# Half of a shift vector moved to another engine and another time, a release order changed, and a last norm split over three engines

## The chip, the cores and the metric

The kernel runs on one core of a Trainium2 chip. Five engines work side by side, each with a queue of its own: PE (TensorE: matrix products), DVE (VectorE), ACT (ScalarE), POOL (GpSimd) and SP (SyncE, which here only issues loads and stores). The metric is device time in microseconds (us), lower is better; executions of one kernel agree closely, and about 0.2% is what can be told from no change.

## The reference

One layer of a hybrid encoder block on 256 tokens of width 2048, all in float32, and a final norm. Cut to what matters:

```python
mod = silu(c) @ w_ada + b_ada                     # 2048 x 12288
sh1, sc1, gt1, sh2, sc2, gt2 = split(mod, 6)
h = rms_norm(x, g_mix) * (1 + sc1) + sh1
qa, ka, va, qb, kb, vb = split(h @ w_in)          # 2048 x 4608
o = concat[rms_norm(attention_A), rms_norm(attention_B)]   # 16 heads each
x = x + gt1 * (o @ w_out)                         # 2048 x 2048
h = rms_norm(x, g_ffn) * (1 + sc2) + sh2
# top-1 of 4 groups, then top-2 of its 8 experts, for each token
y = sum over experts of combine[:, e] * ((silu(h @ w_gate[e]) * (h @ w_up[e])) @ w_down[e])
x = x + gt2 * y
shf, scf = split(silu(c) @ w_ada_final + b_ada_final, 2)   # 2048 x 4096
out = rms_norm(x, g_final) * (1 + scf) + shf
```

Heads of B have a bias by relative position. There are 32 experts, each with three matrices of 4.2 MB.

## The kernel before

**The ring.** All large weights come through one ring of six SBUF buffers of 2.1 MB (`Ring`). The tiles are listed in the order of use; SP issues the loads in that order, and a load waits until the buffer released six tiles before is free. Buffers are freed by PE (products done) or by DVE (sums done), in program order.

**Stages, in order of time.** (1) The first two mod vectors with the first part of W_in, about 0 to 160 us. (2) W_in: twelve steps (`in_step`), each with one tile of w_in (64 or 32 products on PE, about 14 us) and, by the table `VECTOR_TILES`, two further tiles of w_ada or w_ada_final. These extra tiles are worked off on DVE: a vector times a 2048 x 1024 block is 16 scalar_tensor_tensor operations of 128 x 1024 (`vec_step`, L385), four to a tile, into an accumulator that ones-products on PE add up over the partitions later (`vec_finish`, L404). (3) W_out: eight steps (`out_step`) with two halves t = 0, 1 of 16 products each, again with extra tiles. The attention is woven in: `weave(n)` starts n heads' scores, transposes the heads of the weave before and does the value products of the one before that. In W_in a step has `weave(0)` and `weave(2)`; in W_out each half has `weave(2)`. For B a head pair's bias strip is loaded on ACT's queue (`bias_B`), and POOL sets a corner of it (L454) before it scales the heads' probabilities (L494, L495). All heads must be done before W_out's step 4. (4) Routing: router products, second norm (`rsqrt_mean`, L190 to L198, with its Sqrt on ACT, L192), a chain of small DVE operations, then the first gather (L780). (5) MoE: eight groups of four experts. Each group has 16 tiles of gate and up and 8 of down; a group's result is scattered back (`scatter`, L863) while the next group runs. After group 0 a branch (`further_rounds`) is there for experts with more than 32 tokens; it isn't taken with these inputs. (6) The final norm and the output.

**The vector shf** (the first half of w_ada_final's columns, 16.8 MB) is made on PE: its columns 0 to 1535 in eight tiles of 1.6 MB, six before the routing (`shift_step` into the bank `shift`, copied at L692) and two before group 0's experts (`shift_b`); its last 512 columns in three tiles at the very end (`last_block`), behind the last w_down tile. The output of columns 0 to 1535 is normalized and stored before that last block, the rest after it.

**Scatters after group 0** stand before the branch, those of the other groups in the next group's steps. Group 7's w_down tiles hold 128 rows by 1024 columns of four experts.

Of the kernel before, what the change touches and what calls it, by code (L numbers as in the profile page):

```python
# [38 lines left out]
VECTOR_TILES = [2, 2, 2, 2, 2, 2, 2, 2, 2, 2, 2, 2, 2, 2, 2, 2, 3, 3, 2, 0]  # L39
# [45 lines left out]
def block_kernel(ctx: ExitStack, tc: tile.TileContext, a: dict):  # L85
# [25 lines left out]
    for name, w, col in (("gt1", ada, 2 * D), ("sh2", ada, 3 * D), ("sc2", ada, 4 * D), ("gt2", ada, 5 * D), ("scf", fin, D)):  # L111
        for c in (0, 1024):
            vec_tiles += [((name, c // 512), k, 4, 1024, rows(w, k * 512, 4, col + c, 1024)) for k in range(4)]
# [11 lines left out]
    shf_tiles = [ring.add((2, 1536), rows(fin, 256 * i, 2, 0, 1536)) for i in range(8)]  # L125
# [3 lines left out]
    for g in range(8):  # L129
# [18 lines left out]
    last_block = [(c0, c1, ring.add((c1 - c0, 512), rows(fin, c0 * 128, c1 - c0, 1536, 512))) for c0, c1 in ((0, 8), (8, 14), (14, 16))]  # L148

# [61 lines left out]
    with ExitStack() as sa:  # L211
# [384 lines left out]
        def out_step(i, idx):  # L596
# [8 lines left out]
            for t in range(2):  # L605
# [15 lines left out]
                weave(2)  # L621
# [53 lines left out]
        def shift_step(pm, i, last):  # L675
            w = ring.get(shf_tiles[i])
            for k in range(2):
                for J in range(3):
                    PE.matmul(
                        pm[32 * J : 32 * J + 32, :], lhsT=cact[:, 2 * i + k : 2 * i + k + 1].to_broadcast([128, 32]),  # L680
                        rhs=w[:, k, J * 512 : (J + 1) * 512], start=k == 0 and i in (0, 6), stop=k == 1 and i == last, skip_group_check=True,
                    )
            ring.release(shf_tiles[i])

        shift = bank("s", "shift")
        shift_step(shift, 0, 5)
        router_turns(3)
        shift_step(shift, 1, 5)
# [57 lines left out]
        V.tensor_copy(cnt, pp[0:1, 64:96])  # L746

# [59 lines left out]
    def turned(pw, name):  # L807
# [3 lines left out]
        sm = pb.tile([128, SEQ], F32, tag="smat", name=f"smat_{name}")  # L811
# [40 lines left out]
    def gated(yp, ch, name):  # L852
        ys = pb.tile([128, 2, 512], F32, tag="ys", name=f"ys_{name}{ch}")
        for n in range(2):
            c = ch * 1024 + n * 512
            V.tensor_tensor(ys[:, n, :], yp[n], gt2bc[:, c : c + 512], op=ALU.mult)  # L856
        return ys

# [36 lines left out]
    def further_rounds():  # L895

        with tc.If(nc.values_load(most[0:1, 0:1], min_val=0, max_val=2) > 0):
            pke = pb1.tile([128, 2], F32, name="pke")
            cbe = pb1.tile([128, 2], F32, name="cbe")
            with tc.For_i(0, 8, 1) as g, tc.If(nc.values_load(busy[0:1, bass.ds(g, 1)], min_val=0, max_val=2) > 0), tc.For_i(g * 4, g * 4 + 4, 1) as e:  # L900
# [4 lines left out]
                with tc.For_i(0, n_e, 1) as _:  # L905
# [7 lines left out]
                    smf = turned(pwf, "f")  # L913
# [12 lines left out]
                    for ch in range(2):  # L926
# [11 lines left out]
                        scatter(smf, gated(ypf, ch, "f"), ch, "f")  # L938


    four = pb1.tile([128, 2], F32, name="four")
    V.tensor_reduce(four[:, 0:1], ident[:, 0:128:32], axis=AX.X, op=ALU.add)
# [3 lines left out]
    shift = mbank("y", "shift_b", 4)  # L946
    for i in range(6, 8):
        shift_step(shift, i, 7)
    shf_b = pb1.tile([128, 512], F32, name="shf_b")
    S.copy(shf_b[0:96, :], shift[0:96, :])  # L950

# [14 lines left out]
    for g in range(8):  # L966
# [8 lines left out]
        else:  # L975
            for J in range(4):
                steps[(3, 4, 5, 6)[J]].append(lambda J=J: spread([R["gt2"]], ROW_ADA + 20, gt2bc, (J,)))
# [45 lines left out]
        else:  # L1023
            S.activation(four[:, 1:2], four[:, 0:1], AF.Sqrt)
            rl = pb1.tile([128, 512], F32, tag="act", name="rl")
            for ch in range(2):
                yp = [mbank("y", f"yp{g}{ch}{n}", 4) for n in range(2)]
                for fc in range(4):
                    w = ring.get(dn[ch * 4 + fc])
                    down(yp, aT, lambda e: w[:, e, :], fc)  # L1030
                    ring.release(dn[ch * 4 + fc])
                    if fc == 1 and ch == 1:
# [3 lines left out]
                    if fc == 1 and ch == 0:  # L1036
                        shbc = new_xg("shbc").rearrange("p k n -> p (k n)")
                        spread([R["shf"][0:96], shf_b[0:96]], ROW_FIN, shbc, range(3))
                pending.append((sm, gated(yp, ch, f"g{g}"), ch, f"g{g}", True))
        if g == 0:  # L1040
            for job in pending:
                scatter(*job)
            pending = []
            further_rounds()

    tail = mbank("u", "tail", 1)
    PE.matmul(tail, lhsT=pick(ROW_FIN + 3, 128), rhs=pr, start=True, stop=False)  # L1050
    for job in pending:
        scatter(*job)
# [4 lines left out]
    for t in range(2):  # L1057
        for n in range(3):
            c = slice(n * 512, (n + 1) * 512)
            V.scalar_tensor_tensor(big[:, t, c], big[:, t, c], r3[:, t : t + 1], shbc[:, c], op0=ALU.mult, op1=ALU.add)  # L1060
        nc.sync.dma_start(out=out[:, t, 0:1536], in_=big[:, t, 0:1536])
    part = mbank("y", "part", 4)
    for c0, c1, idx in last_block:
        w = ring.get(idx)
        for c in range(c0, c1):
            if c < 14:
                q = 32 * (c % 4)
                PE.matmul(
                    part[q : q + 32, :], lhsT=cact[:, c : c + 1].to_broadcast([128, 32]), rhs=w[:, c - c0, :],
                    start=c < 4, stop=c >= 10, skip_group_check=True,  # L1070
                )
            else:
                PE.matmul(tail, lhsT=cact[:, c : c + 1].to_broadcast([128, 128]), rhs=w[:, c - c0, :], start=False, stop=False)
        ring.release(idx)
        if c1 == 14:
            sums = pb.tile([128, 2, 512], F32, tag="ys", name="sums")[:, 0, :]
            S.copy(sums, part)
    PE.matmul(tail, lhsT=four[:, 0:1].to_broadcast([128, 128]), rhs=sums, start=False, stop=True)
    for t in range(2):
        V.scalar_tensor_tensor(big[:, t, 1536:D], big[:, t, 1536:D], r3[:, t : t + 1], tail, op0=ALU.mult, op1=ALU.add)  # L1080
        nc.sync.dma_start(out=out[:, t, 1536:D], in_=big[:, t, 1536:D])
# [26 lines left out]
```

## Time and profile before

| | |
|---|---|
| median of 3 runs | 1528.02 us (1527.36 to 1528.42) |
| profiled execution | 1529.11 us, span 1527.4 |
| PE busy | 1204.1 us, 79% of the span |
| DVE busy | 480.1 us, 31% |
| ACT, POOL busy | 165.0 and 147.5 us |
| moved by DMA | 599.38 MB, mean 392 GB/s |
| chain that ended last | DMA 44%, PE 10% |

The span is the time from the first to the last instruction in the trace; the profiled execution's own time is 1.7 us more. Busy shares are means over stages with different limits, so the stages have to be read one by one: a stage in which DMA moves data without a pause is bound by the bytes, and one in which it pauses is bound by whoever must free the ring's next buffer. Matmuls are pipelined, and a busy PE is not PE at its peak.

### The profile page before, as it was taken

The page shows a single profiled execution, that of the slowest core. Times are in us where ns is not written, and L with a number is a line of the kernel's source. Part 1 is how long each engine was busy: PE and PEld are TensorE (multiplying, and loading weights), DVE is VectorE, ACT ScalarE, POOL GpSimd, SP SyncE. Part 2 cuts the span into 40 slices and gives each one's busy share as a digit, 9 for nine tenths or more (in the row PEclk, how much of TensorE's full clock was granted, in tenths as well). Part 3 has the DMA queues.
Part 4 walks back from the last instruction along what each step waited for, and adds up shares of the span by engine and source line. Part 5 has one row for each costly group of instructions (what it writes and reads, how often), then busy time and mean ns, then how long its engine had stood idle before and what let it go on. Part 6 is the DMA issues. An engine that isn't in the chain of part 4 may idle for free.

```text
span 1527.4 us, 14326 instructions
## 1 busy us (share of the span) xinstructions
PE 1204.1 (79%) x5975; PEld 531.4 (35%) x5976; DVE 480.1 (31%) x791; ACT 165.0 (11%) x421; POOL 147.5 (10%) x144
## 2 busy tenths in 40 slices
PE   5989999999899977767767667767667767767886
PEld 2777866864444532221212211211211211221221
DVE  1463766755679520120101111101201111111123
ACT  2001122223211110000000100100000000000011
POOL 1000444323431100000000000000000000000002
PEclk9999999999999989888989888889988988897998
DMA  9999999968689899998999999999999999999997
GB/s 339 395 392 401 393 391 365 374 257 337 225 331 403 343 419 421 421 413 359 421 421 421 421 421 422 421 422 421 421 421 421 421 421 421 421 422 422 421 411 303
DMA packets 124173, 599.38 MB, mean 392 GB/s; under 512 B 5864, under 2 KB 8472, under 8 KB 76744
## 3 DMA queue, kind: packets, MB, share of 16 engines
q1 hardware_dynamic: 120384, 595.61, 96.7%
q10 hardware_dynamic: 3688, 2.79, 0.6%
q8 instruction: 48, 0.79, 0.2%
q14 instruction: 21, 0.17, 0.0%
q0 software_dynamic: 32, 0.02, 0.0%
HBM read 596.02 MB, written 2.12 MB: 392 GB/s over the span
## 4 chain that ended last, share of the span: by engine, by line
DMA 44%; PE 10%; DVE 0%; issue 0%; DVEq 0%; ACT 0%; SPq 0%; ACTq 0%
DMA ring<-w_down 23%; DMA ring<-w_up 12%; DMA ring<-w_gate 9%; PE yp L847 5%; PE gp L819 2%; PE up L819 2%; PE sc_g L863 0%; PE bc L760 0%; DVE big L1060 0%; PE bc L761 0%; DVEq L1104 0%; PE tail L1050 0%; ACT rl L867 0%; DVE rl_n L195 0%; DVE x L865 0%
## 5 line engine op out<-in xcount | busy, mean ns | idle before, releaser
L847 PE MATMUL yp<-ring,actT_g 128*32 128x512 f32 x1024 | 182.9, 767 | 101.7 <-DMA ring<-w_down 96.6
L819 PE MATMUL gp<-ring,xg_g 128*32 128x512 f32 x1024 | 180.7, 739 | 73.5 <-DMA ring<-w_gate 73.5
L819 PE MATMUL up<-ring,xg_g 128*32 128x512 f32 x1024 | 172.9, 702 | 68.3 <-DMA ring<-w_up 68.3
L608 PE MATMUL po<-ring,oT 128*128 128x512 f32 x256 | 118.9, 622 | 3.8 <-DMA ring<-w_out 3.8
L847 PEld LDWEIGHTS yp<-ring,actT_g 128*32 128x32 f32 x1024 | 39.4, 134 | 231.0 <-DMA ring<-w_down 133.3
L789 DVE TENSOR_SCALAR xg_g<-g_g,gsc,sh2c 128x128 f32<-128x128 f32 x64 | 26.2, 409 | 294.4 <-PE g_g L780 277.1
L865 DVE TENSOR_TENSOR x<-x,sc_g 128x512 f32<-128x512 f32 x64 | 44.0, 687 | 226.9 <-PE sc_g L863 226.9
L819 PEld LDWEIGHTS gp<-ring,xg_g 128*32 128x32 f32 x1024 | 40.0, 128 | 198.6 <-DMA ring<-w_gate 106.1
L868 POOL TENSOR_TENSOR big<-x,xg_gscf 128x512 f32<-128x512 f32 x8 | 9.9, 1276 | 981.5 <-DVE x L865 981.5
L819 PEld LDWEIGHTS up<-ring,xg_g 128*32 128x32 f32 x1024 | 37.7, 124 | 189.0 <-DMA ring<-w_up 101.0
L787 ACT ACTIVATE xg_g<-g_g,sh2c,gsc 128x128 f32<-128x128 f32 x64 | 29.3, 457 | 506.2 <-DVE xg_g L789 506.2
L385 DVE SCALAR_TENSOR_TENSOR acc_gt<-ring,cact,acc_gt 128x1024 f32<-128x1024 f32 x60 | 82.9, 1382 | 1.6
L856 DVE TENSOR_TENSOR ys_g<-yp,gt2bc 128x512 f32<-128x512 f32 x32 | 21.8, 690 | 169.1 <-PE yp L847 169.1
L608 PEld LDWEIGHTS po<-ring,oT 128*128 128x128 f32 x256 | 50.2, 200 | 67.9 <-issue 63.9
L780 PEld LDWEIGHTS g_g<-pn_g,big 128*128 128x128 f32 x512 | 61.2, 196 | 29.0 <-issue 28.2
L780 PE MATMUL g_g<-pn_g,big 128*128 128x128 f32 x512 | 67.4, 286 | 1.3 <-DVE pn_g L772 1.3
L863 PE MATMUL sc_g<-ys_g,smat_g 128*128 128x512 f32 x128 | 64.6, 631 | 2.1 <-DVE ys_g L856 2.1
L349 PE MATMUL qA<-hT,ring 128*128 128x256 f32 x256 | 61.6, 396 | 4.8 <-DVE hT L344 3.5
L575 PE MATMUL pw_vB<-ring,hT 128*128 128x512 f32 x128 | 58.9, 615 | 0.0
L579 PE MATMUL pw_kB<-hT,ring 128*128 128x256 f32 x256 | 56.9, 381 | 0.0
L579 PE MATMUL pw_qB<-hT,ring 128*128 128x256 f32 x256 | 56.5, 381 | 0.0
L349 PEld LDWEIGHTS qA<-hT,ring 128*128 128x128 f32 x256 | 50.7, 199 | 13.1 <-DVE hT L344 4.3
(331 smaller groups left out, 1095.3 us busy)
## 6 DMA issues: line engine op xcount, KB each, us to landing
ring<-w_gate SPq DMA_DIRECT2D x64, 2048.0 KB, 20.3
ring<-w_up SPq DMA_DIRECT2D x64, 2048.0 KB
ring<-w_down SPq DMA_DIRECT2D x64, 2048.0 KB, 22.0
ring<-w_ada SPq DMA_DIRECT2D x32, 2048.0 KB, 8.3
ring<-w_ada SPq DMA_DIRECT2D x32, 1024.0 KB, 14.1
ring<-w_in SPq DMA_DIRECT2D x12, 2048.0 KB, 15.5
ring<-w_ada_final SPq DMA_DIRECT2D x9, 2048.0 KB
ring<-w_out SPq DMA_DIRECT2D x8, 2048.0 KB, 10.8
```

Source lines behind the costliest of these rows:

```text
L349: PE.matmul(early[n // 2][:, (n % 2) * 256 : (n % 2 + 1) * 256], lhsT=w[:, n * 128 : (n + 1) * 128], rhs=hT[:, kk, :], start=kk == 0 and n ...
L385: V.scalar_tensor_tensor(accs[name], w[:, kk, :], cact[:, c : c + 1], accs[name], op0=ALU.mult, op1=ALU.add)
L575: PE.matmul(b[s], lhsT=hT[:, kk, s * 128 : (s + 1) * 128], rhs=w[:, k, :], start=kk == 0, stop=kk == 15)
L579: PE.matmul(b[s][:, n * 256 : (n + 1) * 256], lhsT=w[:, k, c * 128 : (c + 1) * 128], rhs=hT[:, kk, :], start=kk == 0 and n == 0, stop=kk = ...
L608: PE.matmul(b, lhsT=oT[:, (i // 4) * 8 + k, t * 128 : (t + 1) * 128], rhs=w[:, k, :], start=k == 0, stop=k == 7)
L780: PE.matmul(pm[:, i * 128 : (i + 1) * 128], lhsT=big[:, t, kk * 128 : (kk + 1) * 128], rhs=pn[:, t, :], start=t == 0 and i == 0, stop=t == ...
L787: S.activation(xg[:, kk, :], pm[:, i * 128 : (i + 1) * 128], AF.Identity, bias=sh2c[:, kk : kk + 1], scale=gsc2[:, kk : kk + 1])
L789: V.tensor_scalar(xg[:, kk, :], pm[:, i * 128 : (i + 1) * 128], gsc2[:, kk : kk + 1], sh2c[:, kk : kk + 1], op0=ALU.mult, op1=ALU.add)
L819: PE.matmul(bankt[32 * e : 32 * e + 32, :], lhsT=xg[:, kk, 32 * e : 32 * e + 32], rhs=w[e // 2][:, e % 2, j, :], start=kk == 0, stop=kk == ...
L847: PE.matmul(y[32 * e : 32 * e + 32, :], lhsT=aT[:, fc, 32 * e : 32 * e + 32], rhs=w(e)[:, n * 512 : (n + 1) * 512], start=fc == 0, stop=fc ...
L863: PE.matmul(pm, lhsT=sm[:, t * 128 : (t + 1) * 128], rhs=ys[:, n, :], start=True, stop=True)
L865: V.tensor_tensor(x1[:, t, c], x1[:, t, c], pm, op=ALU.add)
```

## The change

1. shf's columns 1024 to 2047 are made on PE in four tiles of 2.1 MB before the routing; columns 0 to 1023 become a sixth vector of DVE's (four more extra tiles). `VECTOR_TILES` gives W_in's steps 2 and 3 tiles by turns (30 instead of 24) and W_out's 14 instead of 16. `last_block` and `shift_b` are gone.
2. W_out's halves weave one head at t = 0 and two at t = 1.
3. ACT's copy of the shift bank stands behind the routing's position products (L747), not ahead of the Sqrt.
4. Group 0's scatters go into group 1's steps; the branch's body gets buffers of its own.
5. Group 7's last two down tiles hold 256 rows by 512 columns; each is gated and scattered by itself.
6. The final norm goes over four halves: one on ACT (scale) and POOL (add), three on DVE; stores are issued from SP and ACT.

```diff
-VECTOR_TILES = [2, 2, 2, 2, 2, 2, 2, 2, 2, 2, 2, 2, 2, 2, 2, 2, 3, 3, 2, 0]
+VECTOR_TILES = [2, 3, 2, 3, 2, 3, 2, 3, 2, 3, 2, 3, 2, 2, 2, 2, 3, 2, 1, 0]
...
-    shf_tiles = [ring.add((2, 1536), rows(fin, 256 * i, 2, 0, 1536)) for i in range(8)]
+    shf_tiles = [ring.add((4, 1024), rows(fin, 512 * i, 4, 1024, 1024)) for i in range(4)]
...
+            wd = a["w_down"][e0 : e0 + 4].rearrange("e (f p) n -> p e f n", p=128)
             for ch in range(2):
-                for fc in range(4):
-                    src = a["w_down"][e0 : e0 + 4, fc * 128 : (fc + 1) * 128, ch * 1024 : (ch + 1) * 1024].rearrange("e p n -> p e n")
-                    dn.append(ring.add((4, 1024), src))
+                for fc in range(4 - 2 * ch):
+                    dn.append(ring.add((4, 1024), wd[:, :, fc, ch * 1024 : (ch + 1) * 1024]))
+            for n in range(2):
+                c = 1024 + 512 * n
+                dn.append(ring.add((4, 2, 512), [wd[:, :, 2 + f, c : c + 512] for f in range(2)]))
...
-                weave(2)
+                weave(1 + t)
...
-        for i in range(2, 6):
-            shift_step(shift, i, 5)
-        S.copy(R["shf"][0:96, :], shift[0:96, :])
+        for i in (2, 3):
+            shift_step(i)
...
         V.tensor_copy(cnt, pp[0:1, 64:96])
+        S.copy(R["shf"][64:128, :], shift[64:128, :])
...
-                for fc in range(4):
-                    w = ring.get(dn[ch * 4 + fc])
-                    down(yp, aT, lambda e: w[:, e, :], fc)
...
+            scatter(sm, ys, 0, "g7", True)
+            ys = pb.tile([128, 2, 512], F32, tag="ys", name="ys_g71")
+            for n in range(2):
+                w = ring.get(dn[6 + n])
+                for f in range(2):
+                    down(yp[2 + n : 3 + n], aT, lambda e: w[:, e, f, :], 2 + f)
+                ring.release(dn[6 + n])
+                gate(ys, yp[2 + n], 1, n)
+                scatter(sm, ys, 1, "g7", True, ns=(n,))
         if g == 0:
-            for job in pending:
-                scatter(*job)
-            pending = []
             further_rounds()
...
+    for t, ch in ((1, 1), (0, 0), (0, 1), (1, 0)):
+        half = slice(ch * 1024, ch * 1024 + 1024)
+        for c in (slice(ch * 1024, ch * 1024 + 512), slice(ch * 1024 + 512, ch * 1024 + 1024)):
+            if (t, ch) == (1, 1):
+                S.activation(big[:, t, c], big[:, t, c], AF.Identity, scale=r3[:, t : t + 1])
+                G.tensor_tensor(big[:, t, c], big[:, t, c], shbc[:, c], op=ALU.add)
             else:
-                PE.matmul(tail, lhsT=cact[:, c : c + 1].to_broadcast([128, 128]), rhs=w[:, c - c0, :], start=False, stop=False)
...
+                V.scalar_tensor_tensor(big[:, t, c], big[:, t, c], r3[:, t : t + 1], shbc[:, c], op0=ALU.mult, op1=ALU.add)
+        if (t, ch) != (1, 1):
+            (S if ch else nc.sync).dma_start(out=out[:, t, half], in_=big[:, t, half])
+    S.dma_start(out=out[:, 1, 1024:D], in_=big[:, 1, 1024:D])
```

In SP's queue, the loads of W_in's last two steps and of W_out's first tile stood like this (ring is the buffer, then its source; 128x8x512 and 128x4x1024 are both 2.1 MB):

```order
L72 DMA ring_1535<-w_in 128x8x512
L72 DMA ring_1537<-w_ada 128x4x1024
L72 DMA ring_1583<-w_ada 128x4x1024
L72 DMA ring_1638<-w_in 128x8x512
L72 DMA ring_1640<-w_ada 128x4x1024
L72 DMA ring_1693<-w_ada 128x4x1024
L72 DMA ring_1762<-w_out 128x8x512
```

Now they stand like this:

```order
L72 DMA ring_1572<-w_in 128x8x512
L72 DMA ring_1637<-w_ada 128x4x1024
L72 DMA ring_1692<-w_ada 128x4x1024
L72 DMA ring_1694<-w_in 128x8x512
L72 DMA ring_1741<-w_ada 128x4x1024
L72 DMA ring_1760<-w_ada 128x4x1024
L72 DMA ring_1797<-w_ada 128x4x1024
L72 DMA ring_1799<-w_out 128x8x512
```

The step's third extra tile stands ahead of w_out's first, as in five steps before it.

On ACT, at the routing, before (x1t and hT are the last transposed tokens for the router, rl_n the Sqrt of the second norm, eg the group softmax):

```order
L637 ACTIVATE hT<-x1t_2578,gsc_119 128x256
L637 ACTIVATE hT<-x1t_2585,gsc_119 128x256
L692 COPY R_shf<-shift 96x512
L192 ACTIVATE rl_n_2645<-rv_n_2643 128x2
L724 ACT_TABLE_LOAD
L724 ACTIVATE eg<-eg 128x8
```

And now:

```order
L637 ACTIVATE hT<-x1t_2609,gsc_119 128x256
L637 ACTIVATE hT<-x1t_2616,gsc_119 128x256
L192 ACTIVATE rl_n_2665<-rv_n_2663 128x2
L724 ACT_TABLE_LOAD
L724 ACTIVATE eg<-eg 128x8
L747 COPY R_shf<-shift 64x512
```

The copy of the shift bank moved from ahead of the Sqrt to behind the softmax.

On PE, at the end of the program, before (yp the down products, sc_g the scatters, part and tail the last block of shf):

```order
L847 MATMUL yp_5875<-ring_5833,actT_g_5805 32x512 x4
L1050 MATMUL tail<-pr,ident 128x512
L863 MATMUL sc_g_5935<-ys_g_5930,smat_g_5584 128x512
L863 MATMUL sc_g_5940<-ys_g_5930,smat_g_5584 128x512
L863 MATMUL sc_g_5945<-ys_g_5930,smat_g_5584 128x512
L863 MATMUL sc_g_5950<-ys_g_5930,smat_g_5584 128x512
L1068 MATMUL part<-ring_5859,cact 32x512 x8
L1068 MATMUL part<-ring_5869,cact 32x512 x6
L1073 MATMUL tail<-ring_5884,cact 128x512 x2
L1078 MATMUL tail<-sums,four 128x512
```

And now:

```order
L847 MATMUL yp_5816<-ring_5826,actT_g_5806 32x512 x8
L866 MATMUL sc_g_5922<-ys_g_5912,smat_g_5585 128x512
L866 MATMUL sc_g_5927<-ys_g_5912,smat_g_5585 128x512
L847 MATMUL yp_5817<-ring_5837,actT_g_5806 32x512 x8
L866 MATMUL sc_g_5941<-ys_g_5912,smat_g_5585 128x512
L866 MATMUL sc_g_5946<-ys_g_5912,smat_g_5585 128x512
```

Behind the last down tile there are two scatters and nothing of shf.

## Rows read from the trace of the kernel before

**Rows 1.** The page's slices of the span, 38.2 us each: PE busy tenths, HBM rate.

```profile
PE   5989999999899977767767667767667767767886
...
GB/s 339 395 392 401 393 391 365 374 257 337 225 331 403 343 419 421 421 413 359 421 421 421 421 421 422 421 422 421 421 421 421 421 421 421 421 422 422 421 411 303
```

**Rows 2.** Windows: length, PE, PEld, DVE, ACT, POOL busy (count), clock, DMA share, GB/s.

```profile
160.00:220.00 60.00, 60.00 (x294) 46.73 (x294) 41.07 (x79) 15.65 (x55) 27.32 (x23) 1.00 1.03 400
220.00:375.00 155.00, 151.78 (x650) 95.91 (x649) 97.68 (x180) 40.45 (x124) 57.99 (x57) 0.97 0.92 348
375.00:530.00 155.00, 145.37 (x474) 68.76 (x472) 116.76 (x153) 29.32 (x84) 46.65 (x38) 0.94 0.82 311
685.00:695.00 10.00, 10.00 (x70) 2.50 (x72) 0.40 (x2) 0.37 (x1) 0.00 (x0) 0.73 0.45 156
361.30:388.00 26.70, 23.86 (x79) 10.98 (x78) 14.03 (x30) 7.39 (x25) 12.82 (x14) 0.87 0.65 237
388.00:416.70 28.70, 24.61 (x87) 11.59 (x86) 16.44 (x36) 7.98 (x26) 12.71 (x14) 0.88 0.63 233
```

**Rows 3.** Timeline of SP: start, length of the issue, what is loaded.

```profile
309.73 0.37 SPq L72 DMA_DIRECT2D ring<-w_in  x1
...
691.47 0.90 SPq L72 DMA_DIRECT2D ring<-w_up  x2
```

**Rows 4.** The page's DMA issues: count, KB each, median us from issue to landing.

```profile
ring<-w_gate SPq DMA_DIRECT2D x64, 2048.0 KB, 20.3
...
ring<-w_in SPq DMA_DIRECT2D x12, 2048.0 KB, 15.5
```

**Rows 5.** Timeline of PE, W_in to W_out: start, us, what, idle before and its releaser.

```profile
342.80 7.13 PE L575 MATMUL pw_vB<-ring,hT 128*128 128x512 f32 x16
...
361.35 7.03 PE L608 MATMUL po<-ring,oT 128*128 128x512 f32 x16
...
399.94 0.33 PE L502 MATMUL tpB<-ident,stB 128*128 128x128 f32 x1 [3.10 <-POOL stB L494]
...
486.64 9.98 PE L608 MATMUL po<-ring,oT 128*128 128x512 f32 x16 [3.80 <-DMA ring<-w_out]
```

**Rows 6.** Timeline of POOL in W_out.

```profile
399.09 0.20 POOL L454 MEMSET biasB<- 64x128 f32 x1 [9.66 <-DMA biasB<-scratch]
...
434.38 2.24 POOL L613 TENSOR_TENSOR x<-x,hT 128x512 f32<-128x512 f32 x1 [4.88 <-DVE hT L612]
```

**Rows 7.** DVE's groups by form, 160 to 530: busy us, mean ns, idle before.

```profile
L385 DVE SCALAR_TENSOR_TENSOR acc_gt<-ring,cact,acc_gt 128x1024 f32<-128x1024 f32 x55 | 76.5, 1391 | 1.5
```

**Rows 8.** Timelines of PE and ACT at the routing.

```profile
529.35 1.98 PE L649 MATMUL lg<-wr,hT 128*128 128x36 f32 x16
...
538.38 0.58 ACT L692 COPY R_shf<-shift 96x512 f32<-96x512 f32 x1 [9.71 <-PE shift L679]
...
548.13 3.76 PE L780 MATMUL g_g<-pn_g,big 128*128 128x128 f32 x16 [1.30 <-DVE pn_g L772]
...
555.88 3.99 PE L819 MATMUL gp<-ring,xg_g 128*32 128x512 f32 x31
```

**Rows 9.** Timeline of PE in group 0.

```profile
600.05 3.63 PE L819 MATMUL up<-ring,xg_g 128*32 128x512 f32 x28 [1.62 <-DMA ring<-w_up]
```

**Rows 10.** PE at the branch: the timeline, and the branch's line (ns; start).

```profile
669.09 9.32 PE L863 MATMUL sc_g<-ys_g,smat_g 128*128 128x512 f32 x16 [2.13 <-DVE ys_g L856]
...
L897 PEldq COMPARE_BRANCH  x1: 6092/6092/6092, 677.9 to 677.9; - x1
```

**Rows 11.** Timelines of PE, POOL and DVE at the end.

```profile
1506.65 1.92 PE L847 MATMUL yp<-ring,actT_g 128*32 128x512 f32 x16 [1.25 <-DMA ring<-w_down]
...
1511.35 4.98 POOL L868 TENSOR_TENSOR big<-x,xg_gscf 128x512 f32<-128x512 f32 x4 [4.66 <-DVE x L865]
...
1517.06 4.07 DVE L1060 SCALAR_TENSOR_TENSOR big<-big,r_n,xg_shbc 128x512 f32<-128x512 f32 x6
...
1521.05 1.40 DVE L1080 SCALAR_TENSOR_TENSOR big<-big,r_n,tail 128x512 f32<-128x512 f32 x2
```

More of the change, by code (lines that the diff above doesn't have):

```diff
@@ L810, in turned @@
             PE.transpose(pm[:, t * 128 : (t + 1) * 128], pw[:, t, :], ident)
-        sm = pb.tile([128, SEQ], F32, tag="smat", name=f"smat_{name}")
+        sm = pool.tile([128, SEQ], F32, tag="smat", name=f"smat_{name}")
         S.copy(sm, pm[:, 0:SEQ])
@@ L850, in down, with gated, gate @@
                 )
[L852 to L856, printed above, removed]
-        return ys
+    def gated(yp, ch, name, pool=pb):
+        ys = pool.tile([128, 2, 512], F32, tag="ys", name=f"ys_{name}{ch}")
+        for n, y in enumerate(yp):
+            gate(ys, y, ch, n)
+        return ys
+    def gate(ys, y, ch, n):
+        c = ch * 1024 + n * 512
+        V.tensor_tensor(ys[:, n, :], y, gt2bc[:, c : c + 512], op=ALU.mult)
     def scatter(sm, ys, ch, name, last=False, ns=(0, 1)):
@@ L937, in further_rounds @@
                                     )
-                        scatter(smf, gated(ypf, ch, "f"), ch, "f")
-    four = pb1.tile([128, 2], F32, name="four")
-    V.tensor_reduce(four[:, 0:1], ident[:, 0:128:32], axis=AX.X, op=ALU.add)
+                        scatter(smf, gated(ypf, ch, "f", pb1), ch, "f")
+    root = pb1.tile([128, 1], F32, name="root")
     xg = new_xg("g0")
@@ L945, in block_kernel @@
     pending = []
[L946 to L950, printed above, removed]
     def final_scale(b):
@@ L1023, in block_kernel @@
         else:
-            S.activation(four[:, 1:2], four[:, 0:1], AF.Sqrt)
+            S.activation(root, ident[:, 0:1], AF.Sqrt)
             rl = pb1.tile([128, 512], F32, tag="act", name="rl")
-            for ch in range(2):
-                yp = [mbank("y", f"yp{g}{ch}{n}", 4) for n in range(2)]
-                for fc in range(4):
-                    w = ring.get(dn[ch * 4 + fc])
-                    down(yp, aT, lambda e: w[:, e, :], fc)
-                    ring.release(dn[ch * 4 + fc])
-                    if fc == 1 and ch == 1:
-                        for job in pending:
-                            scatter(*job)
-                        pending = []
[L1036 to L1039, printed above, removed]
+            yp = [mbank("y", f"yp{g}{n}", 4) for n in range(4)]
+            for fc in range(4):
+                w = ring.get(dn[fc])
+                down(yp[0:2], aT, lambda e: w[:, e, :], fc)
+                ring.release(dn[fc])
+                if fc == 1:
+                    shbc = new_xg("shbc").rearrange("p k n -> p (k n)")
+                    spread(R["shf"], ROW_FIN, shbc)
+            ys = gated(yp[0:2], 0, "g7")
+            for fc in range(2):
+                w = ring.get(dn[4 + fc])
+                down(yp[2:4], aT, lambda e: w[:, e, :], fc)
+                ring.release(dn[4 + fc])
+            scatter(sm, ys, 0, "g7", True)
[7 more added lines that the diff above has]
+                scatter(sm, ys, 1, "g7", True, ns=(n,))
         if g == 0:
-            for job in pending:
-                scatter(*job)
-            pending = []
             further_rounds()
[L1049 to L1052, printed above, removed]
     sst3 = pb1.tile([128, 2], F32, name="sst3")
```

55 lines of the change are left out of this document (15 added, 40 removed).

## The prediction

> **What bounds the kernel now.** The span is 1527.4 us, and the profiled execution took 1529.1, so 1.7 us lie around it; the median of the runs shown is 1528.0, 1.1 below. I read the slices first, then windows, then the loads' issues and the timelines. The slices show a kernel that streams: from about 555 to 1500 us HBM delivers 421 GB/s in nearly every slice and falls short only near 690 [rows 1]. A 2.1 MB tile costs 4.98 us there. So nothing that an engine saves after 555 counts by itself; what counts is DMA idle time, and the work left after the last weight lands.
>
> The windows give the idle time. With these shorter rows full speed is 400 GB/s (160 to 220), a tile 5.24 us. From 220 to 375 the mean is 348, so 155 x (1 - 348/400) = 20 us are idle; from 375 to 530 it is 311, idle 34.5; together some 54.7. From 685 to 695 it is 156 against 421, idle 6.3 [rows 2]. In all of them the ring is full: the next load waits for a tile to be released.
>
> In the first two W_out steps (26.7 and 28.7 us) PE is busy 23.9 and 24.6, and its granted clock means 0.87 and 0.88, so part of each ran at the lower level, 1.2 GHz instead of 2.4 [rows 2]. A block of 16 products takes 7.03; at 399.94 the transposes wait 3.10 for POOL; at 486.64 the block waits 3.80 for w_out and then, PE having idled, runs 9.98 instead of 7.03 [rows 5]. PE therefore paces W_out, with waits in it.
>
> **The change, part by part.**
>
> *More tiles in W_in.* Four new 2.1 MB tiles of W_shf go through VectorE, and two of the old ones move forward, so six more lie ahead of W_out's first tile: 6 x 5.24 = 31.4 us of DMA. By bytes: 400 x 60 + 348 x 155 = 78 MB come in from 160 to 375 [rows 2], which were the tiles up to the two behind W_out's second. At 400 throughout that is 195 us, so they would be in at 355; in the new list one tile more makes it W_out's first: 360 to 361. It is wanted at 361.35. The last W_in tile is four places ahead, about 340, and wanted at 342.80 [rows 5]; before, it was issued at 309.73 [rows 3], landed some 15.5 us later [rows 4] and so had 17.6 in hand. Most of the 31.4 thus fills idle time and slack. I take W_in 1 us longer; bounds 0 and +16 (none of the 20 usable, 15 in hand).
>
> VectorE: 24 more operations in W_in at 1.391 us [rows 7] are 33 us on some 200; it is 63% busy there (97.7 of 155) [rows 2], so 80%. They hide beside PE, which is 98% busy. Without that cover they would cost 33.
>
> *W_out.* Two tiles fewer, in steps 5 and 6 counted from 0: 8 x 1.39 = 11 us less VectorE work where the load of 486.64 came late. I count that stall as gone: 3.80 + 2.95 = 6.8. `weave(1 + t)` spreads the eight last heads over 3 a step, not 4. The heads' bias strips are loads on ACT's queue, and POOL stands in line behind them: 9.66 us of waiting before 399.09 [rows 6]. The new order puts three such waits at shorter distances, where before there were two, and all heads end only at step 3, so the norm of oB is waited for by the next step. Prices from the two slow steps: PE's loss there was 5 and 7 us against some 22 of work. One more is +6; the norm, +4 with its clock loss. That eats the 6.8 and more; the fewer heads per step give some back. I take 0 for W_out; bounds -18 (all three losses gone) and +12.
>
> *Routing.* ACT's queue held the Sqrt of the second norm behind a copy that waited for all the shift products: the copy starts at 538.38, and the gather comes at 548.13, 9.75 later [rows 8]. Now the copy stands behind the routing. The Sqrt can run as soon as the sum of squares is there, and the last logits decide: they end at 529.35 + 1.98 = 531.3, as before, since the shift products in front of them are 16 instead of 12 or 24. From there Sqrt and small VectorE operations take at most the same 9.75, less the copy's 0.58: the gather at 540. The four products of the half-shift's last tiles hide in that chain. The products of the shift's last two tiles, which stood between the gather's end (551.9) and that block, are gone too, so the first gate block, which ended at 555.88 + 3.99 = 559.9, 11.7 after the gather, ends 7.5 to 9.5 after it: 8.5, and with the 1 us of W_in at 549.5.
>
> What that is worth: the ring holds six MoE tiles by then, and the seventh starts only when this block releases its slots. Before, its start was set by bytes: the twelfth tile landed at 600.05 [rows 9], so the seventh began at 600.05 - 6 x 4.98 = 570.2. Now PE sets it, at 549.5 + 1 for the issue = 550.5. DMA alone could reach 570.2 - 54.7 + 10.5 (4.2 MB that were loaded at the end) = 526, so it isn't in the way. Gain 19.7; bounds 4 (W_in +16) and 38 (W_out -18).
>
> *Further rounds.* After group 0 PE runs eight scatters, 9.32 us from 669.09, then the branch, 6.09 in one COMPARE_BRANCH [rows 10], and SP's next load is issued only at 691.47 [rows 3]. The scatters now go into group 1, where PE has room (busy digits 6 and 7 in the full stream [rows 1]). PE reaches the branch some 10 us earlier and so makes its first release near 681, before the idle stretch. Gain 6.3, the whole idle time; bounds 0 and 6.3. A long jump after a branch is what the Trainium skill (Runtime: NRT & Kernel Launch, Instruction fetch mechanics) would lead one to expect: a taken branch out of the fetched window waits for a fetch. The 6.09 agrees; by that page the jump itself stays, and with it 6 of the 16 us that PE is held.
>
> *The tail.* Before, 4.2 MB of W_shf came behind the last w_down tile and hid most of the last work: that tile starts its products at 1506.65, the norm starts at 1517.06, 10.4 later, and the span ends 20.75 later [rows 11]. Now w_down is last. Of its final tile only half the columns remain: one group of products instead of four (-1.3) and two scatters instead of four (-1.75): norm after 7.35. The norm: six VectorE operations of 0.68 (4.07 for six), and ACT with two POOL additions of 1.25 (4.98 for four) [rows 11]. If POOL runs beside VectorE, the last output leaves 4.1 after the norm's start; if they exclude each other, 4.07 + 2.5 = 6.6. Before it left at 5.4 (VectorE ended at 1522.45), 5 before the end. So 7.35 + 4.1 + 5 to 7.35 + 6.6 + 5 = 16.5 to 19 against 20.75. A POOL addition took 2.24 at 434.38 beside VectorE operations with both operands in SBUF [rows 6], against the 1.25 beside VectorE additions that read a PSUM bank. The norm's operands are all in SBUF, so I go by the 2.24, near the long end: 18, and 0.5 for the 2 KB rows of the last two tiles (4.2 MB at 400 instead of 421). Gain 2.3; bounds 1 and 4.
>
> The Trainium skill (SBUF — State Buffer, SBUF: two separate sides) states a rule that speaks against a third engine here: a VectorE operation with two SBUF inputs and a POOL operation that reads SBUF hold one shared port pair by turns, whole instructions long. The 2.24 agrees. By the rule the tail is 19 and its gain 1.3; by the 1.25 alone it is 16.5 and the gain 3.8.
>
> **Sum.** 19.7 + 6.3 + 2.3 = 28.3. 1529.1 - 28.3 = 1500.8, and against the median 1528.0 - 28.3 = 1499.7; I say 1501.
>
> **The rivals.**
> *W_in becomes the bound.* VectorE at 63% and POOL at 37% (58 of 155) [rows 2] sum to 100%; with the new operations 117%. If they take turns, and part of both is waiting already, 7 to 17% of 200 us are too much: W_in 14 to 34 longer, the time 1515 to 1535; I price it at 1515, since PE was 98% busy at those 100%. Against it: POOL's largest share is small operations. 0.13. The port rule of the Trainium skill (SBUF — State Buffer, SBUF: two separate sides), quoted for the tail, would act in this way.
> *The branch stall stays*, because the jump and not the scatters holds the ring: 28.3 - 6.3, 1507; 0.1 of the forecast's chance.
> *Slower: the bias strips.* They share the DMA engines with the tiles. If in a stream that never pauses a strip lands as late as a tile of the full stream (20.3 us [rows 4]) and not in the 9 or so of POOL's 9.66 [rows 6], the three waits of W_out grow by some 11 each: 33 in all, 1534. It decides from 9.4 more per wait. Against it: that strip too came while tiles were loading. 0.06.
> *No gain:* W_in +16, W_out +12 together: 1529; 0.05.
>
> **How the numbers follow.** Forecast, 1487 to 1513: 0.72. Better than 1487 (W_out without waits): 0.04. W_in bound, 1513 to 1525: 0.13. Near 1528: 0.05. Slower: 0.06. 1487 to 1516 holds the forecast and half of the W_in case, some 0.8. About 0.2%, 3 us, is what a measurement can tell from no change: faster 0.89, within it 0.04, slower 0.07.
>
> **What would show it.** Right: 395 to 400 GB/s from 220 to 345 with W_out starting before 364; the Sqrt within 3 us of the logits and the gather near 540; no slice under 415 near 690; the seventh MoE tile near 550; the end 17 to 19 after the last w_down tile's first product. Wrong: PE waiting for W_in or for strips, W_out past 165 us, the jump still followed by an empty ring.

## The result, and the profile after

| | before | after |
|---|---|---|
| median | 1527.69 us (1527.31 to 1528.42) | 1515.62 us (1512.74 to 1518.00) |
| ratio | | 0.992, 95% interval 0.9901 to 0.9938 |
| profiled execution, span | 1529.11, 1527.4 us | 1515.09, 1513.4 us |

The kernel is 12 us faster; the two spans differ by 14.0. The forecast was 28.3. So the sign was right and more than half of the gain is missing. The page of the changed kernel, slices of 37.8 us (HBM rate), answers to [rows 1]:

```profile
GB/s 335 395 392 400 393 403 403 402 401 400 278 326 322 388 385 420 422 375 423 422 421 422 421 421 421 421 422 421 422 420 421 422 421 421 422 421 422 422 403 173
```

The dip to 257 in the ninth slice of before is gone: W_in now streams without a pause. The dip near the eighteenth slice is still there, and the last slice has fallen from 303 to 173: the end is now work without loads. The windows, against [rows 2]:

```profile
220.00:375.00 155.00, 151.36 (x655) 95.99 (x654) 124.53 (x204) 41.18 (x125) 61.67 (x57) 0.98 1.03 401
375.00:530.00 155.00, 147.56 (x465) 69.82 (x466) 104.09 (x142) 29.09 (x84) 49.63 (x39) 0.95 0.86 330
...
530.00:570.00 40.00, 35.87 (x255) 15.49 (x250) 11.48 (x61) 6.05 (x14) 0.00 (x0) 1.00 0.96 387
...
550.00:555.00 5.00, 5.00 (x52) 2.56 (x43) 1.12 (x3) 0.73 (x2) 0.00 (x0) 1.00 0.72 252
...
660.00:680.00 20.00, 16.64 (x96) 4.60 (x88) 3.10 (x5) 0.00 (x0) 0.00 (x0) 1.00 0.84 337
```

In W_in the rate is 401 (348 before) and VectorE is busy 124.5 of 155 us, the forecast 80%, with PE still at 98%. W_out went from 311 to 330. Behind group 0 (660 to 680) 20 x (1 - 337/421) = 4.0 us are idle, against 6.3 before.

The timeline of PE, from W_out's first block to group 0's last down tile (compare [rows 5] and [rows 8]), and from VectorE's the operation that takes up the position products (pp):

```profile
362.07 7.03 PE L608 MATMUL po<-ring,oT 128*128 128x512 f32 x16
...
417.28 7.03 PE L608 MATMUL po<-ring,oT 128*128 128x512 f32 x16
...
457.90 0.73 PE L536 MATMUL pnB<-ones,sqB 128*128 128x1 f32 x4 [3.12 <-POOL sqB L529]
...
522.88 1.87 PE L649 MATMUL lg<-wr,hT 128*128 128x36 f32 x16
...
529.41 3.63 PE L681 MATMUL shift<-ring,cact 128*32 128x512 f32 x16
532.97 1.98 PE L649 MATMUL lg<-wr,hT 128*128 128x36 f32 x16
534.87 7.06 PE L681 MATMUL shift<-ring,cact 128*32 128x512 f32 x32
541.86 0.41 PE L739 MATMUL pp<-oT,tri 128*128 128x32 f32 x2
...
543.00 0.22 DVE L744 SCALAR_TENSOR_TENSOR posk<-oT,pp 128x64 f32<-128x64 f32 x1 [3.30 <-PE pp L743]
...
544.33 2.02 PE L780 MATMUL g_g<-pn_g,big 128*128 128x128 f32 x16 [1.37 <-DVE pn_g L772]
547.68 3.64 PE L819 MATMUL gp<-ring,xg_g 128*32 128x512 f32 x32 [1.34 <-DVE xg_g L789]
...
645.12 3.63 PE L847 MATMUL yp<-ring,actT_g 128*32 128x512 f32 x28 [1.67 <-DMA ring<-w_down]
```

Three lines of PE's timeline before, for comparison: the third logits, group 0's last w_down tile, and the first block of group 1:

```profile
521.85 1.87 PE L649 MATMUL lg<-wr,hT 128*128 128x36 f32 x16
...
659.68 5.29 PE L847 MATMUL yp<-ring,actT_g 128*32 128x512 f32 x28 [3.36 <-DMA ring<-w_down]
...
685.27 6.15 PE L819 MATMUL gp<-ring,xg_g 128*32 128x512 f32 x32
```

W_out starts 0.7 us later than before (forecast 1). The old stall at 486.64 is gone, and a new one stands at 457.90. Each shift tile takes 3.63 us on PE; the last logits end at 534.95 (forecast 532.3), and the position products stand behind 7.06 us of shift products. The gather comes at 544.33, not 541 (540 and W_in's 1), the first gate block ends at 551.3, not 549.5. The load of group 0's last w_down tile ends PE's wait at 645.12, and at 659.68 before: the stream is 14.6 us ahead there.

At the branch: SP's timeline, and then the instructions of the branch's line (count, duration in ns, first and last start):

```profile
647.96 1.19 SPq L72 DMA_DIRECT2D ring<-w_gate  x2
675.30 0.90 SPq L72 DMA_DIRECT2D ring<-w_up  x2
```

```profile
L900 SPq EVENT_SEMAPHORE  x9: 17/17/17, 655.3 to 675.2; - x9
...
L900 PEldq COMPARE_BRANCH  x1: 6492/6492/6492, 649.3 to 649.3; - x1
```

The same events in the kernel before:

```profile
L897 SPq EVENT_SEMAPHORE  x9: 17/17/17, 671.5 to 689.7; - x9
```

SP issues nothing for 26 us. Its nine semaphore events end at 675.2, just as the last of its outstanding loads have come in (25 GB/s from 674 to 675, none in the next us), so it waits there for its own loads. PE had finished its first block of group 1 at 662.3, 13 us sooner.

The end, timelines of PE, DVE and POOL (before: [rows 11]):

```profile
1480.67 3.64 PE L847 MATMUL yp<-ring,actT_g 128*32 128x512 f32 x16 [3.85 <-DMA ring<-w_down]
1484.24 4.58 PE L866 MATMUL sc_g<-ys_g,smat_g 128*128 128x512 f32 x8
1488.74 1.92 PE L847 MATMUL yp<-ring,actT_g 128*32 128x512 f32 x16
1491.48 1.98 PE L866 MATMUL sc_g<-ys_g,smat_g 128*128 128x512 f32 x4 [0.81 <-DVE ys_g L860]
1493.40 1.92 PE L847 MATMUL yp<-ring,actT_g 128*32 128x512 f32 x16
...
1501.98 6.07 DVE L1058 SCALAR_TENSOR_TENSOR big<-big,r_n,xg_shbc 128x512 f32<-128x512 f32 x6
...
1502.76 3.42 POOL L1056 TENSOR_TENSOR big<-big,xg_shbc 128x512 f32<-128x512 f32 x2 [2.14 <-ACT big L1055]
```

The last two tiles' products (1488.74 and 1493.40) wait for no load: they stand behind scatters on PE. VectorE's six operations take 6.07, where six took 4.07 before; POOL's two 3.42, where four took 4.98.

### The profile page after: what moved, and what is told of

The parts are those of the page before. It is cut to its first block, busy times and chain, and to the rows that moved or that the text cites. A ratio compares the mean times of both kernels' runs of the same rounds, so it can differ in the third digit from the quotient of the medians.

```text
span 1513.4 us, 14209 instructions
## 1 busy us (share of the span) xinstructions
PE 1187.8 (78%) x5909; PEld 525.7 (35%) x5910; DVE 499.3 (33%) x804; ACT 166.9 (11%) x423; POOL 158.6 (10%) x146
## 4 chain that ended last, share of the span: by engine, by line
DMA 44%; PE 10%; DVE 1%; issue 0%; ACT 0%; DVEq 0%; ACTq 0%
DMA ring<-w_down 23%; DMA ring<-w_up 12%; DMA ring<-w_gate 10%; PE yp L847 5%; PE up L819 2%; PE gp L819 2%; PE sc_g L866 1%; DVE big L1058 0%; DVE ys_g L860 0%; DVE rv_n L190 0%; ACT rl L870 0%; DVE x L868 0%; DVEq L1084 0%; ACT rl_n L192 0%; DVE rl_n L197 0%
## 5 line engine op out<-in xcount | busy, mean ns | idle before, releaser
L819 PE MATMUL gp<-ring,xg_g 128*32 128x512 f32 x1024 | 174.8, 713 | 68.8 <-DMA ring<-w_gate 64.1
L385 DVE SCALAR_TENSOR_TENSOR acc_gt<-ring,cact,acc_gt 128x1024 f32<-128x1024 f32 x60 | 78.6, 1309 | 1.6
```

Source lines behind the costliest of these rows:

```text
L385: V.scalar_tensor_tensor(accs[name], w[:, kk, :], cact[:, c : c + 1], accs[name], op0=ALU.mult, op1=ALU.add)
L819: PE.matmul(bankt[32 * e : 32 * e + 32, :], lhsT=xg[:, kk, 32 * e : 32 * e + 32], rhs=w[e // 2][:, e % 2, j, :], start=kk == 0, stop=kk == ...
```

## The experiments

Each kernel is the changed kernel with one edit, unless it says more. A ratio is against the kernel before, measured with it. The intervals are 0.2 to 0.3% to either side, so an edit worth 2 to 4 us is judged by its rows, and its ratio only has to fit.

**after_again.** No edit.

> The changed kernel as it is, for comparison with the others of this call. All theories: 0.992 of the time before, and the same stretches as in its first profile (idle near 670 to 680, norm about 23 us behind the last loads).

0.9925 (0.9895 to 0.9956), 1515.1 us: the result again, and the comparison for what follows. Its 660 to 680 reads 340 GB/s, its norm starts at 1501.95.

**branch_late.** `further_rounds()` moves from behind group 0 into group 7, behind the second down tile; its body gets banks and buffers that are free there.

```diff
-        if g == 0:
-            further_rounds()
...
                 if fc == 1:
+                    further_rounds()
```

> The branch moves from behind group 0 to behind group 7's second down tile, where SP has issued its last load. Theory A, SP's drain: at the branch SP waits until all of its own loads have landed (nine semaphore events, 24.7 us of waiting in the changed kernel), so the ring starts again empty; moved, the 4.0 us of DMA idle time near 670 to 680 go, that stretch reads above 415 GB/s, and the time is 1515.6 - 4.0 = 1511.6. PE's 6 us at the branch are then hidden, since a tile's products there take 1.9 of some 5 us. Theory B, PE's jump of 6 us and what follows it set the loss: it comes back at the new place, the last down products start 4 to 6 us late, and the time stays within 1 us of 1515.6.

0.9899 (0.9879 to 0.9919), 1510.3 us. The window of the old place:

```profile
660.00:680.00 20.00, 16.49 (x94) 4.46 (x98) 2.75 (x4) 0.37 (x1) 0.00 (x0) 0.84 1.01 421
```

The 4.0 us of idle time are gone, as theory A says. PE pays its 6.01 us jump at the new place; no load is held by it there.

**scatter_before.** Group 0's scatters ahead of the branch again.

```diff
         if g == 0:
+            for job in pending:
+                scatter(*job)
+            pending = []
             further_rounds()
```

> Only the scatters of group 0 go back ahead of the branch. The prediction's step (PE's late first release makes the whole stall): 6.3 us come back, 1515.6 + 6.3 = 1521.9. Theory A, SP's drain ends at 675 whatever PE does: PE's first release comes some 2 us behind it and the next ones 3.5 apart, so only 2.3 us come back (idle 6.3 instead of 4.0), 1517.9.

0.9909 (0.9882 to 0.9936), 1512.4 us, and 339 GB/s from 660 to 680: 3.9 us idle, as without the edit. Neither figure came in. The branch's line shows why:

```profile
L900 SPq EVENT_SEMAPHORE  x9: 17/17/17, 657.3 to 677.2; - x9
...
L900 PEldq COMPARE_BRANCH  x1: 352/352/352, 664.0 to 664.0; - x1
```

SP's wait is the same, to 677.2, and its next load is issued at 677.33. PE's jump took 0.35 us in this run, not 6, so PE was not late in spite of its scatters. That SP's drain makes the stall is confirmed; what the scatters cost beside a 6 us jump (at most the 2.3 between 6.3 and 4.0) is left open.

**shift4.** The shift products use all four groups of 32 output columns on PE.

```diff
-                for J in (2, 3):
+                for n in range(2):
+                    q = 32 * (2 * (k % 2) + n)
                     PE.matmul(
-                        shift[32 * J : 32 * J + 32, :], ...
+                        shift[q : q + 32, :], ...
```

> The shift products use four column groups of TensorE instead of two (rows k even in groups 2 and 3, k odd in groups 0 and 1; the two halves are summed when the row is spread). Theory: two column groups side by side run at half the rate of four, so 16 products took 3.63 us instead of 1.8; two such blocks stand ahead of the last logits and two ahead of the position products, for which VectorE waits 3.30 us. Then a block takes 1.8 to 1.9, the gather starts 5.8 us earlier (3.6 + 2.2) at about 538.5, and the time is 1515.6 - 5.8 = 1509.8. Rival: the rate of these products is set by their weight loads or by the clock, not by the column groups; the blocks stay at 3.6 and the time at 1515.6.

0.9892 (0.9867 to 0.9917), 1507.7 us. PE's timeline:

```profile
525.27 1.92 PE L682 MATMUL shift<-ring,cact 128*32 128x512 f32 x16
527.12 1.98 PE L649 MATMUL lg<-wr,hT 128*128 128x36 f32 x16
529.03 3.64 PE L682 MATMUL shift<-ring,cact 128*32 128x512 f32 x32
534.00 0.38 PE L740 MATMUL pp<-oT,tri 128*128 128x32 f32 x2 [1.33 <-DVE oT L737]
...
536.43 2.99 PE L785 MATMUL g_g<-pn_g,big 128*128 128x128 f32 x16 [1.37 <-DVE pn_g L777]
```

A block of 16 takes 1.92 instead of 3.63, and the position products now wait for VectorE and not behind the shift. This run's W_out was 3.3 us earlier already (third logits at 519.61 instead of 522.88); from there to the gather it takes 16.8 us instead of 21.45, so the edit is worth 4.6, not 5.8. Of this the stream gets less: group 0's tenth tile ends PE's wait at 569.32 instead of 575.15, 5.8 sooner with the 3.3 in it, since from 530 to 570 the loads now run at 423 GB/s (387 in the changed kernel) and have no idle time left to fill.

**copy_back.** Part 3 undone: `S.copy(R["shf"]...)` right behind the shift products.

> ACT's copy of the shift bank stands ahead of the second norm's Sqrt again. The prediction's step: the Sqrt then waits for all the shift products (they end near 541.9 in the changed kernel), VectorE's chain starts behind it, and the gather comes at about 553 instead of 544.3; 8.5 us later, 1524. Rival, the chain is set by the position products, which stand behind the same shift products anyway: at most 2 us, 1517.6.

0.9963 (0.9946 to 0.9979), 1520.7 us, 5.7 more than after_again. ACT's and PE's timelines:

```profile
543.54 0.58 ACT L693 COPY R_shf<-shift 64x512 f32<-64x512 f32 x1 [11.41 <-PE shift L681]
544.14 0.20 ACT L192 ACTIVATE rl_n<-rv_n 128x2 f32<-128x2 f32 x1
...
553.47 3.65 PE L780 MATMUL g_g<-pn_g,big 128*128 128x128 f32 x16 [1.36 <-DVE pn_g L772]
```

The Sqrt waits behind the copy. From the last logits' start to the gather it takes 18.9 us (534.53 to 553.47) instead of 11.4: 7.6 of the 8.5. The prediction's step holds. Of the parts undone here this is the one whose undoing costs most; parts 1 and 6 were not undone by themselves.

**weave2.** Part 2 undone.

```diff
-                weave(1 + t)
+                weave(2)
```

> Only W_out's weaves go back to two heads in each half. The prediction set W_out at 0 as a net of new waits and of fewer heads per step. If that holds for each by itself, the time stays within 2 us of 1515.1. If the one-head weave makes the waits that the changed kernel shows in W_out (1.45, 2.48, 0.84 and 3.12, the last for the norm of oB), undoing it gives up to 5 us back: 1510. If the spread heads are what took the old wait of 3.80 and its slow block away, undoing it costs 5: 1520.

0.9861 (0.9841 to 0.9881), 1505.4 us: undoing this part alone is worth 9.6 us. PE's timeline:

```profile
361.03 7.13 PE L608 MATMUL po<-ring,oT 128*128 128x512 f32 x16 [0.63 <-DMA ring<-w_out]
...
416.75 7.03 PE L608 MATMUL po<-ring,oT 128*128 128x512 f32 x16
...
441.81 0.50 PE L536 MATMUL pnB<-ones,sqB 128*128 128x1 f32 x4
442.17 13.98 PE L608 MATMUL po<-ring,oT 128*128 128x512 f32 x32
...
512.85 1.87 PE L649 MATMUL lg<-wr,hT 128*128 128x36 f32 x16
```

The first four of W_out's blocks take 55.7 us with two heads in each half and 55.2 (362.07 to 417.28) with one and two: the number of heads makes no difference there. Both have waits for POOL in this stretch (7.1 us here, 5.9 in the changed kernel) and a granted clock below full (0.93 and 0.83 in the two windows from 361 to 417 here, 0.87 and 0.88 in the changed kernel); that these set PE's time was not tested. So the changed kernel has more heads left behind the fifth block. It still weaves up to the eighth, and then waits for oB's norm, which here comes ahead of the eighth without a wait. From W_out's first block to the third logits it is 151.8 us; 160.8 in the changed kernel and 160.5 before. Of the 9.0 between the first two, 8.8 lie between the fifth block and the ninth (416.75 to about 449.2 here, 417.28 to 458.49 there), the first that needs oB's norm. The eleven traces with the one-head weave have 157.9 to 162.2 us for this stretch and the two with `weave(2)` (here and in best6) 151.8 and 149.3, so the difference is clear of their scatter.

**tail_order.** The first half's scatters ahead of the sixth down tile.

```diff
                 ring.release(dn[4 + fc])
-            scatter(sm, ys, 0, "g7", True)
+                if fc == 0:
+                    scatter(sm, ys, 0, "g7", True)
```

> The four scatters of group 7's first half move ahead of the sixth down tile's products, where PE waits 3.85 us for its load. Theory, PE's order costs in the tail: the seventh tile's products start when it lands and not behind 4.58 us of scatters, the eighth's when it lands (about 1490.6) and not at 1493.4; the norm starts 2.8 us earlier and the time is 1512.8. Rival, the loads of the last two tiles (2 KB rows, 249 to 295 GB/s there) set the end: the products wait for DMA instead, and the time stays within 0.5 us of 1515.6.

0.9926 (0.9899 to 0.9952), 1512.8 us: not to be told from no change. The rows show a part of the theory (PE):

```profile
1486.44 1.06 PE L847 MATMUL yp<-ring,actT_g 128*32 128x512 f32 x8 [1.50 <-DMA ring<-w_down]
1488.32 3.60 PE L866 MATMUL sc_g<-ys_g,smat_g 128*128 128x512 f32 x4 [0.81 <-DVE ys_g L860]
1491.84 1.95 PE L847 MATMUL yp<-ring,actT_g 128*32 128x512 f32 x16
```

The seventh tile's products now wait for their load; its two scatters then run 3.60 instead of 1.98 at a mean granted clock of 0.83 from 1485 to 1495 (0.97 in the changed kernel), PE having idled ahead of them. The norm starts 1.5 us sooner (1500.46), not 2.8.

**tail_1024.** Part 5 undone: eight down tiles of 128 x 1024.

> Group 7's last two down tiles go back to 128 rows by 1024 columns. Theory A, the half-column tiles cost on the DMA side: 249 to 295 GB/s in their stretch; with 4 KB rows the stream stays near 400 to its end and the last bytes land 3 us sooner; the norm starts 10.4 after the last tile's first products (as in the kernel before), so about 3 us sooner in all, 1512.6. Theory B of the prediction, the half-column tiles save work behind the last load (1.3 of products, 1.75 of scatters): back at 1024 columns the end comes 3 us later, 1518.6.

0.9912 (0.9885 to 0.994), 1513.3 us. Its norm starts at 1503.92 in a run whose gather was 2.85 us later than after_again's (547.37 and 544.52), so 0.9 sooner than there. Theory A's first half holds in part: the loads end near 1493, and near 1491.5 in after_again (windows of 1 us), so some 1.4 us sooner but for the 2.85, not 3; an estimate from one pair of traces. The norm gained 0.9, since the last two tiles' products again stood behind 4.50 us of scatters. Theory B's 3 us didn't come.

**norm_psum.** The shift row stays in PSUM for VectorE.

```diff
-V.scalar_tensor_tensor(big[:, t, c], big[:, t, c], r3[:, t : t + 1], shbc[:, c], ...)
+V.scalar_tensor_tensor(big[:, t, c], big[:, t, c], r3[:, t : t + 1], shp[c.start // 512], ...)
```

> The shift row stays in four PSUM banks for VectorE's six operations of the last norm; POOL's half still reads it from SBUF. Theory, VectorE with two SBUF operands and POOL share a port: without the second SBUF operand the six take 0.70 each as in the kernel before (1.40 for two with a PSUM operand), 4.2 us instead of 6.07, POOL's two additions 2.5 instead of 3.42, and the span ends 1.9 us sooner after the norm's start (11.4 to 9.5). Rival, the six are slow because three engines and the first store share the SBUF itself: they stay near 6.

0.9897 (0.9867 to 0.9927), 1510.0 us. DVE and POOL:

```profile
1498.60 4.04 DVE L1069 SCALAR_TENSOR_TENSOR big<-big,r_n,shp 128x512 f32<-128x512 f32 x6
...
1499.38 2.49 POOL L1067 TENSOR_TENSOR big<-big,xg_shbc 128x512 f32<-128x512 f32 x2 [2.14 <-ACT big L1066]
```

4.04 and 2.49, as the theory says; from the norm's start to the span's end (1508.0) 9.4 us instead of 11.4. This is the rule of the Trainium skill (SBUF — State Buffer, SBUF: two separate sides) that the prediction weighed: a VectorE operation with two SBUF inputs and a POOL operation that reads SBUF take turns. The two kernels agree with it, 6.07 with two SBUF inputs and 4.04 with one; in the kernel before, where POOL was idle during the norm, six with two SBUF inputs took 4.07 [rows 11].

**best4 and best5.** branch_late, shift4, tail_order and norm_psum together; best5 has the last tile's products ahead of the seventh's scatters as well.

> Four corrections together: the branch behind the last loads (4.0), the shift products on four column groups (4.6 between the logits and the gather in its own run), the scatters of the first half ahead of the sixth down tile (1.5 to the norm), the shift row in PSUM for VectorE (2.0 behind the norm). If the terms are separate, they add to 12.1 of the changed kernel's 1515.1: 1503.0, 0.9846 of the time before. If the tail's two overlap with each other or the branch's 6 us now fall into a tail that has less slack, 3 of it are lost: 1506, 0.9866.

> As best4, and the last tile's products stand ahead of the seventh tile's scatters. If PE's order in the tail still costs (the last tile's products stood at 1491.84, 3.6 us of scatters behind the seventh's), 1.3 us less than best4, 1501.7. Rival, the last load lands no sooner than that: same as best4, or 0.5 later, since two scatters now come behind it.

0.9859 (0.9836 to 0.9881), 1504.9 us, and 0.986 (0.9838 to 0.9882), 1504.9 us: 10.2 of the 12.1 came, and the order of the last scatters makes no difference that shows. PE's timeline of best4 shows where it is short now: behind the branch the shift banks' products start at 1455.73, after a wait of 5.30 for the jump, and from there to the end no product waits for a load.

**best6.** best4 with `weave(2)`, with two of the four shift banks made in group 7's gate and up steps.

> The four corrections, two heads again in each half of W_out, and two of the four shift rows made in group 7's gate and up steps instead of between its down tiles (behind the branch PE ran without a wait for loads to the end there). If the weave's gain (9.7 in its own run) and the four (10.2 in theirs) are separate stretches, 1515.1 - 19.9 = 1495, 0.979 of the time before. If the loads now bind in W_out and the routing (full speed leaves little idle time there), a third of the weave's gain is lost: 1498, 0.981.

0.9781 (0.9768 to 0.9794), 1494.8 us: 20.2 us below after_again, where 19.9 were expected. Its windows:

```profile
375.00:530.00 155.00, 147.72 (x539) 70.70 (x539) 110.96 (x177) 32.72 (x91) 50.21 (x41) 0.97 0.92 354
530.00:570.00 40.00, 35.09 (x236) 15.65 (x238) 6.00 (x27) 4.64 (x11) 0.00 (x0) 0.92 1.01 421
...
660.00:680.00 20.00, 15.20 (x68) 3.89 (x68) 2.00 (x3) 0.00 (x0) 0.00 (x0) 0.83 1.01 422
```

The stream is full from the routing on. What is left is W_out: 155 x (1 - 354/400) = 18 us idle. This version beats both kernels; parts 3 and 5 of the change and the later scatters of part 4 are in it as they were, part 1 with the products on four column groups.

## Why the prediction was right in sign and wrong in size

| term | forecast | measured | what the runs showed |
|---|---|---|---|
| W_in | -1 | -0.7 | 401 GB/s, PE 98% busy |
| W_out | 0 | -0.3 | 8.7 won, 9.0 lost |
| routing, stream at group 0 (with the two above) | 19.7 | 14.6 | shift products at half rate, W_out's idle time |
| further rounds | 6.3 | 2.3 | SP's drain |
| tail | 2.3 | -2.9 | PE's order, 2 KB rows, a saving that wasn't there, the shared port |
| sum | 28.3 | 14.0 | |

The measured 2.3 is 6.3 - 4.0 of idle time, the tail's -2.9 what remains of 14.0. Three terms failed: the routing by 5.1, the further rounds by 4.0, the tail by 5.2.

**W_in** was right, step by step: the idle 20 us were filled, VectorE at 80%, W_out 0.7 later. The rival of a bound W_in falls: VectorE and POOL sum to 120% of the stretch, and PE still was not held. The rival of late bias strips falls too: POOL's waits for them were 8.82, 8.70 and 5.07 us, none longer than the 9.66 of before.

**W_out** came out at the forecast sum by two large terms that cancel, and in part by luck. The stall's end and the lighter steps gave 8.7 (160.5 to 151.8 with two heads a half; the prediction had 6.8); the one-head weaves took 9.0 (the prediction's price was 10). But that price named strips for 6 of it, and PE's waits for POOL's scaled heads sum to 5.9 us in the changed kernel, 7.1 in weave2: the strips were not it. Its other part, the norm of oB, priced at 4, was (3.12 of waiting, and the longer weave ahead of it).

**Routing: the term was mis-sized.** Two sentences failed. The first is that "the four products of the half-shift's last tiles hide in that chain". They don't: VectorE waited 3.30 us for position products that stood behind 7.06 us of shift products, and the logits behind 3.63. The prediction counted products (16 instead of 12 or 24) and not their rate. The kernel before had a row that gives it, in its groups by form (busy us, mean ns):

```profile
L679 PE MATMUL shift<-ring,cact 128*32 128x512 f32 x72 | 11.7, 595 | 0.0
```

With three column groups in use, 72 products in 11.7 us are 0.163 each. With two it is 3.63 / 16 = 0.227, with four 1.92 / 16 = 0.120: the groups work side by side, and those that aren't used are lost. The Trainium skill (TensorEngine Tiling (Array Packing), Tiling Modes) lists 128 x 32 as four independent tiles; the three numbers agree. With the shift products at half rate the gather came 3.3 us late, and the first gate block ended 1.8 late (551.3 instead of 549.5).

The second is that DMA alone could reach 526, "so it isn't in the way"; the other 3.3 us of the 5.1 lie here. That sum took all 54.7 us of idle time as filled. But W_out at 330 GB/s keeps 155 x (1 - 330/400) = 27 us, and 526 + 27 = 553. So the bytes were as late as PE: when PE released at 551.3, earlier tiles were still landing (172 GB/s from 551 to 552), and SP's next loads came on top (550 to 555 reads 252 GB/s). This is a sum from rows; no run separates the two causes. A term of 0 for W_out's time was no reason to count its idle time as gone.

**Further rounds: the step was wrong.** I took the idle ring for PE's late first release. In the kernel before PE was indeed the later by a little: its first block ends at 685.27 + 6.15 = 691.4, and SP's nine semaphore events at 689.7. That hid the other wait: SP itself stands at the branch until all its loads have landed (no bytes come from 689 to 692). With PE early the stall fell from 6.3 to 4.0; with the branch moved, to nothing. The rival that "the jump and not the scatters holds the ring" was wrong as well: with a jump of 0.35 us, in scatter_before, 3.9 us stayed idle. Nor does the jump itself always stay, as the prediction had it.

**The tail: mis-sized in three places.** By the stream the last tile's products should have started at 1506.65 - 14.6 - 2.3 + 0.5 = 1490.25. They started at 1493.40, 3.15 later. Some 1.2 of this is the loads: they ended near 1491.5, since the 2 KB rows cost more than the 0.5 that the prediction gave them (some 1.4 by tail_1024). The rest is PE's order, the scatters of the tile ahead, which the prediction left out; tail_order won 1.5 of it back. From there to the norm it took 8.58 us instead of 7.35: the prediction's -1.3 for "one group of products instead of four" wasn't there. The last tile has 16 products in 1.92 us in both kernels [rows 11], and only the scatters became fewer. From the norm to the end it took 11.4 instead of 10.65. Together 5.1 of the 5.2 that are missing. The port was in the prediction as a range (4.1 to 6.6 for the norm); 6.07 is near its long end.

Open: why PE's jump took 0.35 us in one of these programs and 6.0 to 6.5 in all others; what half-column tiles are worth once PE's order is out of the way; and what parts 1 and 6 are worth by themselves.

## What to carry to other kernels

Before a stall is given to the engine that ends it, look at the other engines' waits in the same stretch: the later one hides the earlier, and at a branch the queue that issues loads has waits of its own. Price moved PE work by its rate in the new shape (column groups in use) and by what stands behind it on PE, not by its count. A stage forecast at no gain keeps its idle time, and the loads behind it come that much later. Two terms that cancel are worth an experiment each: undoing one line of a change that helped was worth 9.6 us where the whole change gave 12.

## What the runs showed of the hardware

- At a branch whose body isn't run, SP waited 24.7 us until its own outstanding loads had landed; the stream then stood idle for 4.0 us, and for 3.9 in a program in which PE's jump took 0.35 us instead of 6.
- PE's jump there took 6.0 to 6.5 us in all programs but one, and 0.35 in that.
- 16 products of 32 output columns took 3.63 us on two column groups and 1.92 on four.
- Six VectorE operations beside POOL took 6.07 us with both operands in SBUF and 4.04 with one in PSUM; POOL's two, 3.42 and 2.49.
- Four blocks of W_out with eight heads woven in took as long as with six (55.7 and 55.2 us).
